# HGRN scores: the diagonal and the two smallest levels from one product over blocks of four tokens

## The chip, the cores and the metric

The kernel runs on one core of one Trainium2 chip. The time is device microseconds (us) of one launch; a kernel's time is the median of its runs. The engines are named PE (TensorE, matrix products), DVE (VectorE), ACT (ScalarE), POOL (GpSimd) and SP (SyncE, which issues the transfers).

## What is computed

One layer of a hybrid encoder over 16 learned tokens and 256 inputs (272 tokens, width 2048). After an RMSNorm, one projection `w_in` gives the inputs of two mixers: an HGRN2 gated linear recurrence (8 heads of 128) and a diagonal state-space model (S5, 64 groups). Both outputs are normed, joined and projected by `w_out`; a gated MLP with a short convolution and a last RMSNorm follow. The part that the change touches is the score matrix of the recurrence:

```python
f = lb + (1.0 - lb) * sigmoid(z); k = (1.0 - lb) * sigmoid(-z); q = silu(q)
b = cumsum(log(f))                                    # within a chunk
decay = exp(where(causal, b[t] - b[s], -inf))         # = product of f over s+1..t
scores[t, s] = sum_d q[t, d] * k[s, d] * decay[t, s, d]
o_intra = scores @ v
```

## The kernel before

All large products run on PE as three products of split operands (`mm3`, lines 184 to 186: high weights by high input, high by low, low by high). Weights come by DMA into `raw`, in units of 1 MB; `wsplit` makes of each unit two halves of 128x1024: `whi` on ACT (line 160) and `wlo` on DVE (the helper of line 82). Each half then feeds 24 products on PE, eight of them with `wlo`. There are three buffers each for `raw`, `whi` and `wlo`, so that PE can be at most about two halves behind the splits.

The columns of `w_in` are worked through in chunks in the order `u0 h0 u1 h1 u2 h2 u3 h3 g0 g1 g2 g3`. A `u` chunk feeds two S5 tiles (`s5_tile`, tiles `W`, `P`, `m`, `xo`, `bu`, `yps`). An `h` chunk gives two heads: `hg_f` makes the gates `f` (its tile is called `PP` in the profile) and `k`, `hg_q` makes `q`, `hg_i` makes `v`. `hg_group` then makes the 128x128 score blocks `S` (two heads by two blocks of 128 tokens, side by side in 512 columns), and `hg_cross` what crosses the blocks of 128.

`hg_group` never divides. It builds the scores in levels. The diagonal is taken from a product of `k` and `q` (PSUM tile `dps`), masked by the identity. Then, for h = 1, 2, 4, ... 64, blocks of 2h tokens are halved: queries of the right half, scaled by `f` (by then the running product of gates from the start of the half), meet keys of the left half, scaled by `SP` (the running product of gates up to the end of the half). `qh` and `kt` are the scaled operands, `lps` the PSUM tile of the product, and a predicated copy puts it into `S`. At the end of each level two DVE products double the reach of `SP` and of `f`. For h = 1 `SP` is still 1, so `k` itself is used and there is no `kt`.

The order of instructions on each engine is set when the kernel is built, by a scheduler that plays the program against a model of the engines' times, with priorities given in the code (`pri`): weight splits first, then the reading of accumulators, then the work of the heads. On the chip each engine takes its instructions in that fixed order and waits where an operand isn't there.

Of the kernel before, what the change touches and what calls it, by code (L numbers as in the profile page):

```python
# [9 lines left out]
F32 = mybir.dt.float32  # L10
F32R = mybir.dt.float32r
I32 = mybir.dt.int32
# [5 lines left out]
NM = 16  # L18
T = SEQ + NM
# [14 lines left out]
NQ = T - T0  # L34
# [5 lines left out]
NWARM2 = 10  # L40
LATE = 1.003
LEV = [1, 2, 4, 8, 16, 32, 64]

MAGIC = 12582912.0
LOG2E = 1.4426950408889634
# [7 lines left out]

def constants():
    ident = np.eye(128, dtype=np.float32)
    masks = np.zeros((128, len(LEV), 64), np.float32)
    s = np.arange(128)
    for l, h in enumerate(LEV):
        t = np.array([b * 2 * h + h + j for b in range(128 // (2 * h)) for j in range(h)])
        masks[:, l, :] = (s[:, None] // (2 * h) == t[None, :] // (2 * h)) & (s[:, None] % (2 * h) < h)  # L60
    misc = np.zeros((128, 26), np.float32)
    misc[:, 7] = 1.0
    misc[:, 15] = (s // S5H) % 2 == 0
    misc[:, 16] = (s // S5H) % 2 == 1
    misc[:, 17] = (s != NM - 1)
    misc[:, 18:26] = (s[:, None] % 32 == np.arange(NH)) & (s[:, None] < 64)
    return ident, masks.reshape(128, -1), misc
# [3 lines left out]
def hymba_kernel(ctx: ExitStack, tc: tile.TileContext, x, meta, lb_logits, norm_mix, w_in, hg_norm,  # L71
# [4 lines left out]
    act, dve, pool, pe, sp = nc.scalar, nc.vector, nc.gpsimd, nc.tensor, nc.sync  # L76
# [4 lines left out]
    def tt(dst, a, b, op, eng=dve):  # L81
        eng.tensor_tensor(out=dst, in0=a, in1=b, op=op)  # L82
# [21 lines left out]
    MUL, ADD, SUB, MAX, MIN = ALU.mult, ALU.add, ALU.subtract, ALU.max, ALU.min  # L104

    const = ctx.enter_context(tc.tile_pool(name="const", bufs=1))
# [3 lines left out]
    resp = ctx.enter_context(tc.tile_pool(name="res", bufs=1))  # L110

    ident = const.tile([128, 128], F32, name="ident")
    masks = const.tile([128, len(LEV), 64], F32, name="masks")
    misc = const.tile([128, 26], F32, name="misc")
    ones = const.tile([128, 128], F32, name="ones")
    onehot = misc[:, 0:15]
# [226 lines left out]
    def st(nm, p=prm, tag=None):  # L343
# [3 lines left out]
                    in_=lrow[64:96].unsqueeze(2).to_broadcast([32, 2, S5P]))  # L347
# [135 lines left out]
    for ri in range(2):  # L483
        for hb in range(2):
# [4 lines left out]
            for g in range(2):  # L489
                pr = slice(64 * g, 64 * g + 64)  # L490
                act.copy(out=cq[ri][pr, hb * 16:(hb + 1) * 16, :],
                         in_=tp[pr].rearrange("p b (j g h) -> p (b j) g h", g=2, h=S5H)[:, :, g])
# [20 lines left out]
    hgp = hgs.enter_context(tc.tile_pool(name="hg", bufs=1))  # L513
# [116 lines left out]
    oT = ogp.tile([128, NH, NQ], F32, tag="oT", name="oT")  # L630
    gs = ogp.tile([128, NH, NQ], F32, tag="gs", name="gs")
    kts = [hgp.tile([128, 4, 128], F32, name=f"kt{i}") for i in range(2)]
    for k in kts:
        pool.memset(k, 0.0)

    def hg_f(h0, accs):
# [39 lines left out]
            stt(gs[:, h0 + m], accs[m], vcol[:, V_HG + h0 + m:V_HG + h0 + m + 1], sg[:, m], MUL, MUL)  # L676

    def hg_group(h0, f, k, q, v, vm):
        S = hgp.tile([128, 4, 128], F32, tag="S", name="S")
        SP = hgp.tile([128, 2, T], F32, tag="SP", name="SP")  # L680
        pool.memset(SP, 1.0)
        ps = psc.tile([128, 4, 128], F32, tag="sc", name="dps")
        for m in range(2):
            for b in range(2):
                pe.matmul(ps[:, m * 2 + b], k[:, m, NM + 128 * b:NM + 128 * (b + 1)],
                          q[:, m, 2 + 128 * b:2 + 128 * (b + 1)], start=True, stop=True)
        tt(S, ps, ident.unsqueeze(1).to_broadcast([128, 4, 128]), MUL)
        q4 = q[:, :, 2:NQ]
        for l, h in enumerate(LEV):
            nb = 256 // (2 * h)  # L690
            qh = hgp.tile([128, 2, nb, h], F32, tag="qh", name="qh", bufs=3)
            tt(qh, q4.rearrange("p m (n s t) -> p m n s t", s=2, t=h)[:, :, :, 1],
               f[:, :, NM:T].rearrange("p m (n s t) -> p m n s t", s=2, t=h)[:, :, :, 1], MUL)
            if h == 1:
                lhs = [k[:, m, NM + 128 * b:NM + 128 * (b + 1)] for m in range(2) for b in range(2)]
            else:
                kt = kts[l % 2]
                tt(kt.rearrange("p (m b) t -> p m (b t)", b=2).rearrange("p m (n s t) -> p m n s t", s=2, t=h)[:, :, :, 0],
                   k[:, :, NM:T].rearrange("p m (n s t) -> p m n s t", s=2, t=h)[:, :, :, 0],
                   SP[:, :, NM:T].rearrange("p m (n s t) -> p m n s t", s=2, t=h)[:, :, :, 0], MUL)  # L700
                lhs = [kt[:, i] for i in range(4)]
            ps = psc.tile([128, 4, 64], F32, tag="sc", name="lps")
            qf = qh.rearrange("p m n t -> p (m n t)")
            if h >= 32:

                for b0 in range(0, 128, 2 * h):
                    for i in range(4):
                        pe.matmul(ps[b0:b0 + h, i, 0:h], lhs[i][:, b0:b0 + h],
                                  qf[:, 64 * i + b0 // 2:64 * i + b0 // 2 + h], start=True, stop=True)
                    act.copy(out=S[b0:b0 + h, :, b0 + h:b0 + 2 * h], in_=ps[b0:b0 + h, :, 0:h])  # L710
            else:
                for i in range(4):
                    pe.matmul(ps[:, i], lhs[i], qf[:, 64 * i:64 * (i + 1)], start=True, stop=True)  # L713
                nb1 = 128 // (2 * h)
                mk = masks[:, l].bitcast(I32).rearrange("p (n t) -> p n t", t=h)
                dve.copy_predicated(
                    out=S.rearrange("p b (n s t) -> p b n s t", s=2, t=h)[:, :, :, 1],
                    mask=mk.unsqueeze(1).to_broadcast([128, 4, nb1, h]),
                    data=ps.rearrange("p b (n t) -> p b n t", t=h))

            t0 = 0 if 2 * h <= NM else NM
            fv = f[:, :, t0:T].rearrange("p m (n s t) -> p m n s t", s=2, t=h)
            sv = SP[:, :, t0:T].rearrange("p m (n s t) -> p m n s t", s=2, t=h)
            n = (T - t0) // (2 * h)
            tt(sv[:, :, :, 0], sv[:, :, :, 0], fv[:, :, :, 1, h - 1:h].to_broadcast([128, 2, n, h]), MUL)
            tt(fv[:, :, :, 1], fv[:, :, :, 1], fv[:, :, :, 0, h - 1:h].to_broadcast([128, 2, n, h]), MUL)
        return S, SP

    def hg_cross(h0, f, f15, k, q, v, vm, S, SP):
        kx = hgp.tile([128, 2, 128], F32, tag="qh", name="kx", bufs=3)  # L730
        tt(kx, k[:, :, NM:NM + 128], SP[:, :, NM:NM + 128], MUL)
        km = hgp.tile([128, 2, NM], F32, tag="km", name="km")
        tt(km, k[:, :, 0:NM], SP[:, :, 0:NM], MUL)
        qm = hgp.tile([128, 2, NQ], F32, tag="qm", name="qm")
        qx = hgp.tile([128, 2, 128], F32, tag="qh", name="qx", bufs=3)
        tt(qm[:, :, 2:130], q[:, :, 2:130], f[:, :, NM:NM + 128], MUL)
        tt(qx, q[:, :, 130:NQ], f[:, :, NM + 128:T], MUL)
        tt(qm[:, :, 130:NQ], qx, f[:, :, NM + 127:NM + 128].to_broadcast([128, 2, 128]), MUL)
        tt(qm[:, :, 0:1], q[:, :, 0:1], f15, MUL)
        dve.tensor_copy(out=qm[:, :, 1:2], in_=q[:, :, 1:2])  # L740
        ps = psc.tile([128, 2, 128], F32, tag="sc", name="xps")
        for m in range(2):
            pe.matmul(ps[:, m], kx[:, m], qx[:, m], start=True, stop=True)
        sx = hgp.tile([128, 2, 128], F32, tag="sx", name="sx")
        act.copy(out=sx, in_=ps)
        sm = hgp.tile([NM, 2, NQ], F32, tag="iv", name="sm")
        for m in range(2):
            ps = psc.tile([128, NQ], F32, tag="sc", name="mps")
            pe.matmul(ps[0:NM], km[:, m], qm[:, m], start=True, stop=True)
            act.copy(out=sm[:, m, 1:NQ], in_=ps[0:NM, 1:NQ])  # L750
            ts(sm[:, m, 0:1], ps[0:NM, 0:1], misc[0:NM, 17:18], MUL)
        for m in range(2):
            ps = psc.tile([128, NQ], F32, tag="sc", name="ops")
            pe.matmul(ps, vm[:, m], sm[:, m], start=True, stop=False)
            pe.matmul(ps[:, 2:130], v[:, 2 * m], S[:, 2 * m], start=False, stop=False)
            pe.matmul(ps[:, 130:NQ], v[:, 2 * m], sx[:, m], start=False, stop=False)
            pe.matmul(ps[:, 130:NQ], v[:, 2 * m + 1], S[:, 2 * m + 1], start=False, stop=True)
            act.copy(out=oT[:, h0 + m], in_=ps)
# [57 lines left out]
    for c in range(4):  # L816
# [3 lines left out]
        with pri(-3):  # L820
            for m in range(2):
                j = 2 * c + m
                sg = tlp.tile([128, NQ], F32, tag="sq", name="sgl", bufs=3)
# [67 lines left out]
    for c in range(8):  # L891
# [3 lines left out]
        for m in range(2):  # L895
            kt = 2 * c + m
# [21 lines left out]
    for c in range(FF // 256):  # L918
        accs = [pf.tile([128, NQ], F32, tag="f", name="ga") for _ in range(2)]
        mm3(accs, [(wunit(colunit(w_gate, k, c)), k * 8) for k in range(2)], ffr, 0, NQ)  # L920
        for m in range(2):
            j = 2 * c + m
            a = fw.tile([128, NQ], F32, tag="a", name="a", bufs=2)
            b = fw.tile([128, SEQ], F32, tag="b", name="b", bufs=2)
# [23 lines left out]
    for t in range(2):  # L948
        for n in range(4):
            for k in range(4):  # L950
                kt = n * 4 + k
                pe.matmul(dps[t][n][:, k * 128:(k + 1) * 128], hT[:, kt, 2 + t * 128:2 + (t + 1) * 128], ident,
                          start=(k == 0), stop=False, is_transpose=True, skip_group_check=True)
# [18 lines left out]
    for j in range(KF - NT):  # L972
        a = act_split(j)
# [73 lines left out]
```

## Time and profile before

| | |
|---|---|
| runs | 1252.16, 1253.86, 1254.13 us; median 1253.86 us |
| the profiled execution's own time | 1252.36 us |
| its span, first to last instruction | 1250.6 us |
| busy share of the span | PE 98%, DVE 70%, ACT 48%, POOL 9% |
| mean granted TensorE clock | 0.994 |

In the profile's rows a line number is followed by the engine, the operation, the tiles (written tile, arrow, read tiles) and the shape. Many DVE operations come from helpers: line 82 is any product or difference of two tensors, so the tiles tell which it is. A product of two float32 operands on PE stands as two records. Two DVE records that follow each other overlap by some tens of nanoseconds, so what an instruction costs the queue is the distance from its start to the next start. The four heads' groups run between about 65 and 360 us of the span; the MLP fills the span from about 520 us on.

### The profile page before, as it was taken

Reading aid. Unit: us, or ns where it says so; the run is one execution under the profiler, and the core shown is the slowest. Engines: PE = TensorE matmul, PEld = TensorE weight load, DVE = VectorE, ACT = ScalarE, POOL = GpSimd, SP = SyncE. Lnnn points to the kernel's source line nnn. Section 1 sums busy time; section 2 is a strip of 40 time slices with the busy share of each in tenths; the row PEclk is TensorE's granted clock in tenths of the full one; section 3 lists DMA queues with packets and bytes.
Section 4 is the critical chain, followed back from the end, with each engine's and each line's share of the span. In section 5 each row is a group of like instructions: output and inputs, shape, how many; then the busy total and the mean of one; then the engine's idle time right before and its main releaser. Section 6 shows DMA issues by size and latency. Waiting matters only on the chain.

```text
span 1250.6 us, 22795 instructions
## 1 busy us (share of the span) xinstructions
PE 1226.9 (98%) x9299; PEld 1151.9 (92%) x9299; DVE 873.7 (70%) x1516; ACT 601.2 (48%) x1042; POOL 117.0 (9%) x165
## 2 busy tenths in 40 slices
PE   7989999999999999999999999999999999999997
PEld 6979898989989999999999999999999988888886
DVE  8989999999748867765665656656656645554554
ACT  5646767574545446343433433433434434444454
POOL 5483132221000000000000000000000000000000
PEclk9989999999999999999999999999999999999999
DMA  8533344243444565565556555555555545555552
GB/s 256 147 122 113 105 144 136 86 134 127 144 135 136 169 201 172 167 203 179 192 172 199 171 196 173 193 178 187 184 181 191 210 166 198 202 188 187 197 205 98
DMA packets 176298, 210.82 MB, mean 169 GB/s; under 512 B 14773, under 2 KB 168880, under 8 KB 170416
## 3 DMA queue, kind: packets, MB, share of 16 engines
q1 hardware_dynamic: 175871, 209.26, 51.1%
q8 instruction: 73, 1.20, 0.4%
q14 instruction: 34, 0.27, 0.1%
q0 software_dynamic: 320, 0.09, 0.0%
HBM read 206.12 MB, written 2.10 MB: 166 GB/s over the span
## 4 chain that ended last, share of the span: by engine, by line
PE 92%; DVE 3%; POOL 2%; issue 1%; DMA 1%; ACT 0%; SPq 0%; DVEq 0%; ACTq 0%; POOLq 0%
PE acc L186 9%; PE acc L184 8%; PE acc L185 8%; PE ua L185 7%; PE ua L184 7%; PE ga L184 7%; PE ua L186 7%; PE ga L186 7%; PE ga L185 7%; PE d L970 6%; PE d L969 6%; PE d L968 6%; PE lps L713 1%; PE bu L600 1%; DVE xn L91 1%
## 5 line engine op out<-in xcount | busy, mean ns | idle before, releaser
L82 DVE TENSOR_TENSOR wlo<-raw,whi 128x1024 fp32r<-128x1024 f32 (+1 forms) x376 | 461.4, 1227 | 320.8 <-ACT whi L160 271.2
L160 ACT CAST whi<-raw 128x1024 fp32r<-128x1024 f32 (+1 forms) x382 | 397.8, 1042 | 519.9 <-PE ga L185 158.3
L184 PE MATMUL ga<-fh,whi 128*128 128x258 f32 x704 | 199.0, 283 | 0.5 <-DVE a L82 0.5
L186 PE MATMUL ga<-fh,wlo 128*128 128x258 f32 x704 | 198.5, 282 | 0.0
L185 PE MATMUL ua<-fl,whi 128*128 128x256 f32 x704 | 198.4, 282 | 0.0
L185 PE MATMUL ga<-fl,whi 128*128 128x258 f32 x704 | 198.1, 281 | 0.0
L186 PE MATMUL ua<-fh,wlo 128*128 128x256 f32 x704 | 197.9, 281 | 0.0
L184 PE MATMUL ua<-fh,whi 128*128 128x256 f32 x704 | 197.9, 281 | 0.0
L186 PE MATMUL acc<-xh,wlo 128*128 128x272 f32 (+1 forms) x640 | 186.7, 294 | 5.0 <-DVE wlo L82 5.0
L185 PE MATMUL acc<-xl,whi 128*128 128x272 f32 (+1 forms) x640 | 186.1, 292 | 3.9 <-DVE xl L82 3.9
L184 PE MATMUL acc<-xh,whi 128*128 128x272 f32 (+1 forms) x640 | 186.4, 294 | 0.4 <-ACT PP L79 0.4
L184 PEld LDWEIGHTS ga<-fh,whi 128*128 128x128 f32 x704 | 133.0, 189 | 0.7 <-DVE a L82 0.7
L185 PEld LDWEIGHTS ga<-fl,whi 128*128 128x128 f32 x704 | 133.5, 190 | 0.0
L184 PEld LDWEIGHTS ua<-fh,whi 128*128 128x128 f32 x704 | 133.1, 189 | 0.0
L186 PEld LDWEIGHTS ua<-fh,wlo 128*128 128x128 f32 x704 | 132.9, 189 | 0.0
L185 PEld LDWEIGHTS ua<-fl,whi 128*128 128x128 f32 x704 | 132.8, 189 | 0.0
L186 PEld LDWEIGHTS ga<-fh,wlo 128*128 128x128 f32 x704 | 132.6, 189 | 0.0
L186 PEld LDWEIGHTS acc<-xh,wlo 128*128 128x128 f32 x640 | 121.4, 190 | 9.4 <-DVE wlo L82 5.6
L185 PEld LDWEIGHTS acc<-xl,whi 128*128 128x128 f32 x640 | 121.6, 190 | 7.5 <-DVE xl L82 4.8
L968 PE MATMUL d<-whi,ah 128*128 128x512 f32 x328 | 127.7, 389 | 0.0
L969 PE MATMUL d<-whi,al 128*128 128x512 f32 x328 | 127.6, 389 | 0.0
L184 PEld LDWEIGHTS acc<-xh,whi 128*128 128x128 f32 x640 | 121.1, 190 | 4.1 <-issue 2.0
(381 smaller groups left out, 1868.1 us busy)
## 6 DMA issues: line engine op xcount, KB each, us to landing
raw<-in_w_ffn_gate SPq DMA_DIRECT2D x44, 1024.0 KB, 5.1
raw<-in_w_ffn_up SPq DMA_DIRECT2D x44, 1024.0 KB, 5.1
raw<-in_w_ffn_down SPq DMA_DIRECT2D x44, 1024.0 KB, 4.8
raw<-in_w_in SPq DMA_DIRECT2D x39, 1024.0 KB, 5.2
raw<-in_w_out SPq DMA_DIRECT2D x16, 1024.0 KB, 5.8
raw<-in_w_glu SPq DMA_DIRECT2D x4, 1024.0 KB, 5.2
x<-in_x SPq DMA_DIRECT2D x4, 512.0 KB, 5.7
out<-ob SPq DMA_DIRECT2D x8, 256.0 KB, 2.7
```

Of the source, the lines that this page charges most:

```text
L82: eng.tensor_tensor(out=dst, in0=a, in1=b, op=op)
L91: dve.scalar_tensor_tensor(out=dst, in0=a, scalar=s, in1=b, op0=op0, op1=op1, **kw)
L160: act.copy(out=hi[:, c], in_=raw[:, hf, c])
L184: pe.matmul(accs[m], lh, xh[:, n0:n1], start=first, stop=False)
L185: pe.matmul(accs[m], lh, xl[:, n0:n1], start=False, stop=False)
L186: pe.matmul(accs[m], ll, xh[:, n0:n1], start=False, stop=end)
L600: return pe.matmul(bus[i][:, ri], bt[h, 2 * ri + q0 // 2], R[h, q0 // 2], start=True, stop=True)
L713: pe.matmul(ps[:, i], lhs[i], qf[:, 64 * i:64 * (i + 1)], start=True, stop=True)
L968: pe.matmul(dps[t][n], ah[:, tk], hi, start=False, stop=False, skip_group_check=True)
L969: pe.matmul(dps[t][n], al[:, tk], hi, start=False, stop=False, skip_group_check=True)
L970: pe.matmul(dps[t][n], ah[:, tk], lo, start=False, stop=end, skip_group_check=True)
```

## The change

Diagonal, h = 1 and h = 2 become one product. `f` and `SP` are first widened twice (`widen(1)`, `widen(2)`), so that they hold running products within blocks of four tokens. All keys are scaled by `SP` into `kt` (512 columns), all queries by `rv`, the reciprocal of `SP`, into `qt`; inside a block of four, the ratio of two suffix products is the product of the gates between the two tokens. One product of `kt` and `qt` fills `dps`, and one predicated copy with a causal mask of four-token blocks puts it into `S`. The levels h = 4 to 64 stay. The first `SP` is copied from `f` on ACT in place of a DVE product with ones; `S` is one tile that POOL clears once; the mask constant has five in place of seven blocks of 64 columns. `rv` and `qt` lie in the buffers of `qm` and `sg`.

```diff
-    masks = np.zeros((128, len(LEV), 64), np.float32)
+    masks = np.zeros((128, 5, 64), np.float32)
+    masks[:, 0:2] = ((s[:, None] // MBLK == s[None, :] // MBLK) & (s[:, None] <= s[None, :])).reshape(128, 2, 64)
...
-    for k in kts:
+    S = hgp.tile([128, 4, 128], F32, name="S")
+    for k in kts + [S]:
         pool.memset(k, 0.0)
...
+        def widen(h):
+            t0 = 0 if 2 * h <= NM else NM
+            fv, sv = halves(f, h, t0), halves(SP, h, t0)
+            n = (T - t0) // (2 * h)
+            if h == 1:
+                act.copy(out=sv[:, :, :, 0], in_=fv[:, :, :, 1])
+            else:
+                tt(sv[:, :, :, 0], sv[:, :, :, 0], fv[:, :, :, 1, h - 1:h].to_broadcast([128, 2, n, h]), MUL)
+            tt(fv[:, :, :, 1], fv[:, :, :, 1], fv[:, :, :, 0, h - 1:h].to_broadcast([128, 2, n, h]), MUL)
+        widen(1)
+        widen(2)
+        kt = kts[0]
+        qt, rv = (hgp.tile([128, 2, 256], F32, tag=t_, name=n_) for t_, n_ in (("sg", "qt"), ("qm", "rv")))
+        dve.reciprocal(out=rv, in_=SP[:, :, NM:T])
+        tt(kt.rearrange("p (m b) t -> p m (b t)", b=2), k[:, :, NM:T], SP[:, :, NM:T], MUL)
+        tt(qt, q[:, :, 2:NQ], rv, MUL)
         ps = psc.tile([128, 4, 128], F32, tag="sc", name="dps")
         for m in range(2):
             for b in range(2):
-                pe.matmul(ps[:, m * 2 + b], k[:, m, NM + 128 * b:NM + 128 * (b + 1)],
-                          q[:, m, 2 + 128 * b:2 + 128 * (b + 1)], start=True, stop=True)
-        tt(S, ps, ident.unsqueeze(1).to_broadcast([128, 4, 128]), MUL)
-        for l, h in enumerate(LEV):
+                pe.matmul(ps[:, m * 2 + b], kt[:, m * 2 + b], qt[:, m, 128 * b:128 * (b + 1)], start=True, stop=True)
+        dve.copy_predicated(out=S, mask=masks[:, 0:2].bitcast(I32).rearrange("p a t -> p (a t)").unsqueeze(1)
+                            .to_broadcast([128, 4, 128]), data=ps)
+        for l, h in enumerate((4, 8, 16, 32, 64)):
...
-            if h == 1:
-                lhs = [k[:, m, NM + 128 * b:NM + 128 * (b + 1)] for m in range(2) for b in range(2)]
...
+            widen(h)
```

The scheduler gives every engine a new order. Three places matter below.

DVE in the first group (h0), before: from the second `q` to the next weight split. `sca`, `cpc` and `ew` are set-up of the S5 part.

```order
L91 SCALAR_TENSOR_TENSOR q<-acc,lbc,sg 128x258
L82 TENSOR_TENSOR cpc<-sca 128x32x16
L82 TENSOR_TENSOR qh<-q,PP 128x256
L82 TENSOR_TENSOR qm<-q,f_1196 128x2
L740 COPY qm<-q 128x2
L82 TENSOR_TENSOR sca<-scb,zai 128x512
L82 TENSOR_TENSOR sca<-scb,zar 128x512
L82 TENSOR_TENSOR PP<-PP 128x272
L472 COPY ew<-pw 128x32 x3
L82 TENSOR_TENSOR wlo<-raw,whi 128x1024
```

The same place after the change:

```order
L94 SCALAR_TENSOR_TENSOR q<-acc,lbc,sg 128x258
L85 TENSOR_TENSOR cpc<-sca 128x32x16
L85 TENSOR_TENSOR PP<-PP 128x136x2
L705 RECIPROCAL rv<-SP 128x512
L85 TENSOR_TENSOR kt_610<-k,SP 128x512
L85 TENSOR_TENSOR kt_611<-k,SP 128x64x4
L85 TENSOR_TENSOR sca<-scb,zai 128x512
L85 TENSOR_TENSOR sca<-scb,zar 128x512
L85 TENSOR_TENSOR qh<-q,PP 128x256
L475 COPY ew<-pw 128x32 x2
L85 TENSOR_TENSOR wlo<-raw,whi 128x1024
```

The reciprocal and two `kt` products now stand ahead of that split; two small operations on `qm` are gone from there, and `qh` is now that of h = 4.

DVE in the second group (h1), after the change, between two weight splits:

```order
L85 TENSOR_TENSOR wlo<-raw,whi 128x1024
L85 TENSOR_TENSOR PP<-PP 128x136x2
L705 RECIPROCAL rv<-SP 128x512
L85 TENSOR_TENSOR kt_610<-k,SP 128x512
L85 TENSOR_TENSOR kt_611<-k,SP 128x64x4
L85 TENSOR_TENSOR P<-W,m 128x544
L85 TENSOR_TENSOR ysb<-ysb,gq 128x2x129
L94 SCALAR_TENSOR_TENSOR W<-W,pw,tmp 128x2x34
L85 TENSOR_TENSOR P<-W,bu 128x544
L85 TENSOR_TENSOR wlo<-raw,whi 128x1024
```

Eight instructions stand between the two splits, the reciprocal among them.

PE in the first group, before, around the first piece of `dps`:

```order
L185 MATMUL acc<-xl,whi 128x272
L186 MATMUL acc<-xh,wlo 128x272
L685 MATMUL dps<-q,k 128x128 x2
L184 MATMUL acc<-xh,whi 128x272
L185 MATMUL acc<-xl,whi 128x272
```

And after the change, where `dps` now stands: behind the first products with the `wlo` that the DVE rows above end with (the row ahead of `dps` belongs to the unit after it).

```order
L188 MATMUL acc<-xl,whi 128x272
L711 MATMUL dps<-qt,kt_610 128x128 x4
L189 MATMUL acc<-xh,wlo 128x272
L187 MATMUL acc<-xh,whi 128x272
L188 MATMUL acc<-xl,whi 128x272
```

Its two pieces, which stood ahead of that `wlo` among products of earlier halves, are now one piece behind it.

More of the change, by code (lines that the diff above doesn't have):

```diff
@@ L42 @@
 LEV = [1, 2, 4, 8, 16, 32, 64]
+MBLK = 4
 MAGIC = 12582912.0
@@ L55, in constants @@
     ident = np.eye(128, dtype=np.float32)
-    masks = np.zeros((128, len(LEV), 64), np.float32)
+    masks = np.zeros((128, 5, 64), np.float32)
     s = np.arange(128)
-    for l, h in enumerate(LEV):
+    masks[:, 0:2] = ((s[:, None] // MBLK == s[None, :] // MBLK) & (s[:, None] <= s[None, :])).reshape(128, 2, 64)
+    for l, h in enumerate((4, 8, 16)):
         t = np.array([b * 2 * h + h + j for b in range(128 // (2 * h)) for j in range(h)])
-        masks[:, l, :] = (s[:, None] // (2 * h) == t[None, :] // (2 * h)) & (s[:, None] % (2 * h) < h)
+        masks[:, 2 + l, :] = (s[:, None] // (2 * h) == t[None, :] // (2 * h)) & (s[:, None] % (2 * h) < h)
     misc = np.zeros((128, 26), np.float32)
@@ L112, in hymba_kernel @@
     ident = const.tile([128, 128], F32, name="ident")
-    masks = const.tile([128, len(LEV), 64], F32, name="masks")
+    masks = const.tile([128, 5, 64], F32, name="masks")
     misc = const.tile([128, 26], F32, name="misc")
@@ L678, in hg_group, with halves @@
     def hg_group(h0, f, k, q, v, vm):
-        S = hgp.tile([128, 4, 128], F32, tag="S", name="S")
         SP = hgp.tile([128, 2, T], F32, tag="SP", name="SP")
         pool.memset(SP, 1.0)
+        def halves(a, h, t0=NM):
+            return a[:, :, t0 - (T - a.shape[2]):].rearrange("p m (n s t) -> p m n s t", s=2, t=h)
+        def widen(h):
[14 more added lines that the diff above has]
+        tt(qt, q[:, :, 2:NQ], rv, MUL)
         ps = psc.tile([128, 4, 128], F32, tag="sc", name="dps")
@@ L684, in hg_group @@
             for b in range(2):
-                pe.matmul(ps[:, m * 2 + b], k[:, m, NM + 128 * b:NM + 128 * (b + 1)],
-                          q[:, m, 2 + 128 * b:2 + 128 * (b + 1)], start=True, stop=True)
-        tt(S, ps, ident.unsqueeze(1).to_broadcast([128, 4, 128]), MUL)
-        q4 = q[:, :, 2:NQ]
-        for l, h in enumerate(LEV):
+                pe.matmul(ps[:, m * 2 + b], kt[:, m * 2 + b], qt[:, m, 128 * b:128 * (b + 1)], start=True, stop=True)
+        dve.copy_predicated(out=S, mask=masks[:, 0:2].bitcast(I32).rearrange("p a t -> p (a t)").unsqueeze(1)
+                            .to_broadcast([128, 4, 128]), data=ps)
+        for l, h in enumerate((4, 8, 16, 32, 64)):
             nb = 256 // (2 * h)
             qh = hgp.tile([128, 2, nb, h], F32, tag="qh", name="qh", bufs=3)
-            tt(qh, q4.rearrange("p m (n s t) -> p m n s t", s=2, t=h)[:, :, :, 1],
-               f[:, :, NM:T].rearrange("p m (n s t) -> p m n s t", s=2, t=h)[:, :, :, 1], MUL)
-            if h == 1:
-                lhs = [k[:, m, NM + 128 * b:NM + 128 * (b + 1)] for m in range(2) for b in range(2)]
[L696 to L701, printed above, removed]
+            tt(qh, halves(q, h)[:, :, :, 1], halves(f, h)[:, :, :, 1], MUL)
+            kt = kts[(l + 1) % 2]
+            tt(halves(kt.rearrange("p (m b) t -> p m (b t)", b=2), h)[:, :, :, 0],
+               halves(k, h)[:, :, :, 0], halves(SP, h)[:, :, :, 0], MUL)
             ps = psc.tile([128, 4, 64], F32, tag="sc", name="lps")
@@ L707, in hg_group @@
                     for i in range(4):
-                        pe.matmul(ps[b0:b0 + h, i, 0:h], lhs[i][:, b0:b0 + h],
+                        pe.matmul(ps[b0:b0 + h, i, 0:h], kt[:, i, b0:b0 + h],
                                   qf[:, 64 * i + b0 // 2:64 * i + b0 // 2 + h], start=True, stop=True)
@@ L712, in hg_group @@
                 for i in range(4):
-                    pe.matmul(ps[:, i], lhs[i], qf[:, 64 * i:64 * (i + 1)], start=True, stop=True)
+                    pe.matmul(ps[:, i], kt[:, i], qf[:, 64 * i:64 * (i + 1)], start=True, stop=True)
                 nb1 = 128 // (2 * h)
-                mk = masks[:, l].bitcast(I32).rearrange("p (n t) -> p n t", t=h)
+                mk = masks[:, 2 + l].bitcast(I32).rearrange("p (n t) -> p n t", t=h)
                 dve.copy_predicated(
@@ L719, in hg_group @@
                     data=ps.rearrange("p b (n t) -> p b n t", t=h))
[L721 to L726, printed above, removed]
+            widen(h)
         return S, SP
```

## The prediction

> **What bounds the kernel now.** I read the page first, then busy time by stretch, then what PE waited for.
>
> ```profile
> PE 1226.9 (98%) x9299; PEld 1151.9 (92%) x9299; DVE 873.7 (70%) x1516; ACT 601.2 (48%) x1042; POOL 117.0 (9%) x165
> ```
>
> ```profile
> 100.00:300.00 200.00, 200.00 (x1787) 181.30 (x1787) 193.53 (x421) 132.12 (x376) 54.81 (x63) 1.00 0.39 119
> 300.00:400.00 100.00, 100.00 (x810) 92.00 (x808) 72.09 (x134) 49.23 (x87) 1.14 (x2) 1.00 0.46 148
> 81.00:89.50 8.50, 8.50 (x48) 8.00 (x49) 7.82 (x16) 6.48 (x19) 5.72 (x11) 0.50 0.58 179
> ```
>
> The columns of the second fence are the stretch, its length, then busy time of PE, PE's weight loads, DVE, ACT and POOL, and the granted clock. In the stretch where the heads are worked, 100 to 300 us, PE is never idle, but DVE has only 200 - 193.5 = 6.5 us free. In the next 100 us it has 27.9. So two engines are nearly full at once, and the question is which of them sets the pace. The view of PE's waits from 28 to 420 us answers it:
>
> ```profile
> PE acc L186 <- DVE wlo L82: 5.2, 4, 3.6
> PE dps L685 <- DVE q L91: 0.6, 1, 0.6
> ```
>
> Between 90 and 404 us the same view names no wait of PE at all. PE sets the pace, and DVE keeps just ahead of it. The one large wait lies in the first group:
>
> ```profile
> 77.08 0.29 PE L185 MATMUL acc<-xl,whi 128*128 128x272 f32 x1
> 80.97 0.60 PE L186 MATMUL acc<-xh,wlo 128*128 128x272 f32 x1 [3.61 <-DVE wlo L82]
> ```
>
> After it PE runs at half clock until about 89.5 us (the 0.50 above). Anything that makes PE's list shorter behind 81 us is gained in full; anything that keeps DVE from that split at 80 us is lost in full.
>
> **What PE saves.** Each group loses two levels of four products (h = 1, h = 2), eight records each. One level in the second group:
>
> ```profile
> 155.92 0.29 PE L184 MATMUL acc<-xh,whi 128*128 128x272 f32 x1
> 156.05 1.00 PE L713 MATMUL lps<-qh,k 128*128 128x64 f32 x8
> 156.86 0.38 PE L185 MATMUL acc<-xl,whi 128*128 128x272 f32 x1
> 157.07 0.29 PE L186 MATMUL acc<-xh,wlo 128*128 128x272 f32 x1
> ```
>
> 156.05 to 156.86 is 0.81 us, and the product behind it takes 0.21 us to its successor, where the one ahead takes 0.13: 0.89 us a level. Eight levels: 7.1 us. `dps` stays as four products of the same shape. In the first group, however, its two pieces stood ahead of the long wait, where PE's time was free:
>
> ```profile
> 68.67 0.60 PE L685 MATMUL dps<-q,k 128*128 128x128 f32 x4
> 69.03 0.37 PE L184 MATMUL acc<-xh,whi 128*128 128x272 f32 x1
> ```
>
> 0.36 us and the same 0.08 for the product behind, twice. Now they stand behind the wait: +0.9 us.
>
> **What DVE pays.** Of the reciprocal there are only small ones; of the rest there are rows of the same kind.
>
> ```profile
> L780 DVE RECIPROCAL f<-PP 128x2 f32<-128x2 f32 x4 | 0.6, 150 | 0.0
> L439 DVE RECIPROCAL lq<-lq 128x8 f32<-128x8 f32 x1 | 0.2, 191 | 0.0
> L414 DVE RECIPROCAL den<-den 128x32 f32<-128x32 f32 x1 | 0.3, 347 | 0.0
> ```
>
> ```profile
> 153.38 0.68 DVE L82 TENSOR_TENSOR S<-dps,ident 128x512 f32<-128x512 f32 x1
> 153.98 0.24 DVE L91 SCALAR_TENSOR_TENSOR W<-W,pw,tmp 128x34 f32<-128x34 f32 x1
> ...
> 154.48 0.41 DVE L82 TENSOR_TENSOR qh<-q,PP 128x256 f32<-128x256 f32 x1
> 154.81 0.43 DVE L82 TENSOR_TENSOR SP<-SP,PP 128x272 f32<-128x272 f32 x1
> 155.16 0.43 DVE L586 TENSOR_TENSOR_SCAN m<-r,m 128x136 f32<-128x136 f32 x1
> ...
> 157.85 0.41 DVE L82 TENSOR_TENSOR kt<-k,SP 128x256 f32<-128x256 f32 x1
> 158.19 0.71 DVE L82 TENSOR_TENSOR P<-W,m 128x544 f32<-128x544 f32 x1
> ...
> 160.59 0.73 DVE L716 COPY_PREDICATED S<-masks,lps 128x256 f32<-128x256 int32 x1
> 161.12 0.47 DVE L82 TENSOR_TENSOR qh<-q,PP 128x256 f32<-128x256 f32 x1
> ```
>
> From start to start a group loses: `S` from `dps` 0.60, two predicated copies 1.06, two `qh` 0.66, one `kt` 0.34, the first `SP` 0.35; together 3.0 us. It gains `kt` and `qt` of 512 columns (0.60 each, as the `S` product), a predicated copy of 512 columns (between 0.60, the `S` product, which also reads 512 columns of PSUM, and 1.06, twice the row; I take 0.60) and the reciprocal. The three reciprocals lie on one line: (347 - 191) / 24 = 6.5 ns and (191 - 150) / 6 = 6.8 ns for each further column. So 512 columns take 347 + 480 x 6.5 = 3.47 us. The lower bound is the 0.60 of a product, if a long one ran at that pace; the upper is the whole 347 ns scaled by 16, 5.55 us. I take 3.4 in the queue, because the slope holds twice. DVE's account is then +5.2 - 3.0 = +2.2 us a group, 8.8 us in four. It is covered by the 6.5 us free until 300 us and the 27.9 us behind; without that cover all 8.8 would be PE's wait.
>
> [...]
>
> **Where that lands in the first group.** The rows of DVE ahead of the late split:
>
> ```profile
> 70.66 1.76 DVE L82 TENSOR_TENSOR wlo<-raw,whi 128x1024 fp32r<-128x1024 f32 x1
> ...
> 72.74 0.68 DVE L82 TENSOR_TENSOR cpc<-sca 128x512 f32<-128x512 f32 x1
> 73.34 0.42 DVE L82 TENSOR_TENSOR qh<-q,PP 128x256 f32<-128x256 f32 x1
> ...
> 73.93 1.58 DVE L82 TENSOR_TENSOR sca<-scb,zai 128x512 f32<-128x512 f32 x1
> 75.44 1.58 DVE L82 TENSOR_TENSOR sca<-scb,zar 128x512 f32<-128x512 f32 x1
> 76.95 0.56 DVE L82 TENSOR_TENSOR PP<-PP 128x272 f32<-128x272 f32 x1
> 78.94 0.86 DVE L472 COPY ew<-pw 128x32 f32<-128x32 f32 x3 [1.43 <-POOL pw L82]
> 79.70 1.21 DVE L82 TENSOR_TENSOR wlo<-raw,whi 128x1024 fp32r<-128x1024 f32 x1
> ```
>
> and POOL and ACT rows that the walk and the next part use:
>
> ```profile
> 51.59 0.30 POOL L82 TENSOR_TENSOR pt<-pw 128x64 f32<-128x64 f32 x1 [11.06 <-DVE pw L82]
> ...
> 73.89 2.58 POOL L82 TENSOR_TENSOR scb<-ew,pw 128x512 f32<-128x512 f32 x2
> ...
> 85.15 0.36 ACT L658 COPY iv<-acc 128x272 f32<-128x272 f32 x1
> ```
>
> By the new order: up to 73.34 as now (one `kt` is gone ahead of it, two half-size products come); `PP` 0.36, reciprocal 3.4, `kt` 0.60 and 0.34 end at 78.0; then two `sca`. These took 1.51 us each beside POOL's row of 73.89; undisturbed they are 0.60 like `S`. Then `qh` 0.33, two `ew` about 0.5, the split 1.14. It ends at 81.2 with quick `sca` and 83.0 with slow ones, against 80.84. DVE's 1.43 us of waiting for POOL and POOL's drag on `sca` are what covers most of the reciprocal. I take the middle, 82.1: PE resumes 1.3 us later. Bounds: with a reciprocal of 0.60 the split waits for POOL as it does now, 0; with 5.55 it is 3.4.
>
> **Edits that cost nothing.** POOL's clearing of `S` comes once, ahead of the 11.06 us in which POOL waits for DVE; without that wait it would hold POOL for some tenths of a us. The copy of the first `SP` moves to ACT, 132 of 200 us busy, four times about the 0.36 us of the row above; the next `PP` product waits for it, and behind that the reciprocal, so an ACT queue that is late by 1 us would cost 1 us in the first group alone. The mask transfer shrinks. `qt` in the buffer of `sg` and `rv` in that of `qm` add waits on readers that are done microseconds earlier.
>
> **Later groups.** In h1 the row of instructions shown in the order is 0.35 + 3.4 + 0.60 + 0.34 + 0.63 + 0.34 + 0.2 + 0.63 + 1.13 = 7.6 us from split to split, where PE uses up a half in 24 x 0.13 = 3.1 us. The lead there is, from the end of a split to its first product (eight such products a half, counted in order):
>
> ```profile
> 137.72 1.22 DVE L82 TENSOR_TENSOR wlo<-raw,whi 128x1024 fp32r<-128x1024 f32 x1
> ...
> 145.22 0.29 PE L186 MATMUL acc<-xh,wlo 128*128 128x272 f32 x1
> ```
>
> That is 145.22 - 138.94 = 6.3 us. 6.3 + 3.1 - 7.6 leaves 1.8, so PE doesn't wait; the scheduler has moved S5 work behind. Cost: 0, with 1.8 us to spare.
>
> **Sum.** -7.1 + 0.9 + 1.3 = -4.9 us: 1247.5 us for the profiled execution, whose own 1252.36 lies 1.5 below the median of the runs shown. Against the median of 1253.86: 1249.0 us.
>
> **Rivals.**
> A. *DVE's lead isn't there* (the other side). Were the lead in h1 to h3 only what it is in the first group, where the split of 70.66 ends at 72.42 and is first used at 73.67 (row below), then 7.6 - 3.1 - 1.25 = 3.25 us of waiting in each of three groups, 9.75 us: -4.9 + 9.75 = +4.85, 1258.7 us. The change is slower if the lead falls below 4.5 - 4.9 / 3 = 2.9 us. For it: DVE has 6.5 free of 200 us. Against: the 6.3 measured at this place.
>
> ```profile
> 73.67 0.29 PE L186 MATMUL acc<-xh,wlo 128*128 128x272 f32 x1
> ```
>
> B. *The half clock lasts longer.* In the trace it ends 8.5 us after PE resumes. If the later resumption cost another such stretch at half speed, 4.25 us: -0.65, 1253.2 us. For it: PE stands still longer, since `dps` no longer breaks the wait. Against: the stretch may simply move with the resumption. [...]
> C. *The reciprocal is quick* (0.60 us): no later split, -7.1 + 0.9 = -6.2, 1247.7 us. Against: the slope.
> D. *The splits set the pace* and PE's shorter list only becomes waiting: the first split's +1.3 remains (1255.2 us), and DVE's 8.8 come on top as far as the free 6.5 us don't take them, 2.3: 1257.5 us. For it: DVE is busy 97% of 100 to 300 us. Against: no wait of PE between 90 and 404 us.
>
> **How the numbers follow.** About 0.2% (2.5 us) is what a measurement of this kernel can tell from no change. Forecast 0.58; A 0.11, B 0.13, C 0.10, D 0.08. Faster: nearly all of the forecast (0.56), C, and a small part of B (0.03): 0.69. Slower: A and most of D (0.07): 0.18. Same: the rest, 0.13, most of it B. The range: at the low end C's 1247.7 less 1.7, the distance of the fastest of the three runs from their median: 1246.0. At the high end it takes in B, and the forecast with the reciprocal's upper bound and a wait of one group: 1249.0 + 2.1 + 3.25 = 1254.4. A and D (0.19) lie outside.
>
> **What would show it.** Right: the two levels gone from PE's records, PE without waits from about 92 to 404 us, one reciprocal of about 3.5 us a group, PE's long wait ending at 81 to 83 us, DVE busier by some 9 us before 360. Wrong: waits of PE for `wlo` in h1 to h3 (A, D), half clock past 90 us (B), reciprocals below 1 us (C).

## The result, and the profile after

The changed kernel took 1246.05 us in the median (1245.26 to 1247.16, four runs) against 1253.04 us before (1252.16 to 1254.13, four runs): a ratio of 0.9944, 95% interval 0.9927 to 0.9962. It is 7.0 us faster; 4.9 had been forecast. The profiled execution took 1245.69 us, 6.67 less than that of before. Of the experiments below, one run of `pin_copy` (1595.42 us) and one of `pin_warm` (2387.4 us) were slow; without them their medians are 1245.10 and 1245.19 us, and the ratios leave them out.

The page's first part, busy time with its share and the number of instructions:

```profile
PE 1219.3 (98%) x9235; PEld 1144.6 (92%) x9235; DVE 881.3 (71%) x1504; ACT 601.2 (48%) x1046; POOL 116.9 (9%) x166
```

PE has 64 records and 7.6 us less, DVE 7.6 us more. Busy time by stretch, for the same three stretches as before (stretch, length, PE, weight loads, DVE, ACT, POOL, granted clock):

```profile
81.00:89.50 8.50, 7.04 (x40) 7.04 (x41) 7.76 (x16) 3.90 (x13) 6.92 (x11) 0.63 0.62 205
100.00:300.00 200.00, 200.00 (x1767) 182.70 (x1766) 194.16 (x391) 130.39 (x357) 48.93 (x59) 1.00 0.40 125
300.00:400.00 100.00, 99.81 (x809) 89.33 (x807) 81.77 (x162) 53.78 (x116) 6.45 (x6) 1.00 0.42 133
```

PE is still never idle from 100 to 300 us. DVE's added work shows from 300 to 400: 81.8 us instead of 72.1; from 100 to 300 it is 0.6 us more. In the first stretch the clock is 0.63 instead of 0.50. What PE waited for, from 28 to 420 us:

```profile
PE acc L189 <- DVE wlo L85: 7.3, 4, 6.4
PE acc L188 <- DVE xl L85: 2.2, 2, 1.7
PE acc L187 <- ACT PP L82: 0.4, 1, 0.4
```

The one long wait is still that of the first group, 6.4 us instead of 3.6. Between 90 and 404 us the view names only one wait, of 0.2 us, at 398, in another stage. The rows of DVE and PE around the long wait:

```profile
73.79 3.34 DVE L705 RECIPROCAL rv<-SP 128x512 f32<-128x512 f32 x1
77.06 2.04 DVE L85 TENSOR_TENSOR kt<-k,SP 128x512 f32<-128x512 f32 x2
79.02 0.88 DVE L85 TENSOR_TENSOR sca<-scb,zai 128x512 f32<-128x512 f32 x1
79.82 0.69 DVE L85 TENSOR_TENSOR sca<-scb,zar 128x512 f32<-128x512 f32 x1
...
81.19 1.21 DVE L85 TENSOR_TENSOR wlo<-raw,whi 128x1024 fp32r<-128x1024 f32 x1
```

```profile
75.80 0.29 PE L188 MATMUL acc<-xl,whi 128*128 128x272 f32 x1
82.46 0.59 PE L189 MATMUL acc<-xh,wlo 128*128 128x272 f32 x1 [6.37 <-DVE wlo L85]
...
87.96 1.06 PE L711 MATMUL dps<-qt,kt 128*128 128x128 f32 x8
```

The reciprocal takes 3.34 us, the `sca` products behind it run at 0.7 to 0.9 us (POOL's `scb` row is over by 76.6 us), and PE resumes at 82.46 us. `dps` follows behind the wait.

**Where the time went.** Two tables are worked out from the rows of PE. The first gives the time from each product's start to the next one's, added up by the tile written (a wait counts to the product ahead of it), from the 145th to the 2065th weight product (about 44 to 390 us); the second how much later than in the kernel before the n-th weight product (counted from 0) starts:

```
us by tile written     before   after  pe_only  pin_copy  pin_warm
weight products (acc)  261.29  261.75   261.19    261.01    254.34
lps                     23.16   15.59    15.46     15.59     15.60
dps                      3.01    3.52     3.18      3.52      3.52
all else                59.00   58.55    58.84     58.55     65.27
sum                    346.46  339.41   338.67    338.67    338.73
```

```
n (time in before)      after  pe_only  early_b  early_r34
 144  (43.7 us)         +0.35    +1.17    +0.69     +1.26
 288  (64.4 us)         +0.21    +1.17    +0.53     +1.51
 432  (98.5 us)         -1.71    -2.86   -11.90    -10.59
1968 (378.1 us)         -6.70    -6.62    -5.96    -11.53
2352 (430.1 us)         -6.70    -6.63    -7.45    -11.76
last (1225.9 us)        -6.71    -6.66    -7.36    -11.81
```

(In `pin_warm`, experiment 4, all else holds the products added there. Between the rows shown the second table can mislead, since the heads' products stand in other places among the weight products.) The whole gain is there by 378 us and nothing changes behind it. It is `lps`, 7.6 us. Of these, 1.1 us belong to the half clock: in the kernel before, the h = 1 level of the first group ran in it and took 1.90 us from start to start, where the level in the forecast's rows took 0.81:

```profile
84.57 1.97 PE L713 MATMUL lps<-qh,k 128*128 128x64 f32 x8
86.47 0.45 PE L550 MATMUL ktp<-cp,eb 128*32 128x32 f32 x12
```

The weight products cost about the same in sum, because the longer wait (+2.8 us) is balanced by shorter ones ahead of it (-0.8), by less half clock behind it (-0.7) and by 0.8 less further on, where fewer of them stand behind a level. The clock record of the traces has the half clock in steps of 3.41 us (three before, two after), which the expectations call windows:

```
half clock from 76 to 92 us    from    to     length  PE's wait ahead of it
before                         79.48   89.72   10.24   3.6
after                          80.42   87.25    6.83   6.4
pe_only                        81.36   88.19    6.83   3.6
no_recip                       84.79   88.20    3.41   1.7 and 2.8
bwarm                          81.47   91.71   10.24   2.8
pin_copy                       79.52   86.35    6.83   5.8
warm, pin_warm                 none             0      1.2, 1.3
```

### The profile page after: what moved, and what is told of

Same layout as the page of the kernel before. It is cut to its first block, busy times and chain, and to the rows that moved or that the text cites. A ratio compares the mean times of both kernels' runs of the same rounds, so it can differ in the third digit from the quotient of the medians.

```text
span 1243.9 us, 22660 instructions
## 1 busy us (share of the span) xinstructions
PE 1219.3 (98%) x9235; PEld 1144.6 (92%) x9235; DVE 881.3 (71%) x1504; ACT 601.2 (48%) x1046; POOL 116.9 (9%) x166
## 4 chain that ended last, share of the span: by engine, by line
PE 94%; DVE 4%; DMA 0%; issue 0%; ACT 0%; SPq 0%; DVEq 0%; ACTq 0%
PE acc L189 9%; PE acc L187 9%; PE acc L188 9%; PE ua L188 7%; PE ua L187 7%; PE ga L187 7%; PE ua L189 7%; PE ga L189 7%; PE ga L188 7%; PE d L983 6%; PE d L981 6%; PE d L982 6%; PE bu L603 1%; PE lps L732 1%; DVE wlo L85 1%; DVE xn L94 1%
```

## The experiments

Theory P is the forecast's: PE's list sets the time, and only the first group's late split holds it up. The rivals are D (DVE's splits set the pace), O (the gain is a matter of the new order) and H, on the clock: the half clock explains what the sum lacked.

**1. Only PE's products taken out of the kernel before** (`pe_only`).

```diff
-            ps = psc.tile([128, 4, 64], F32, tag="sc", name="lps")
+            if h > 2:
+                ps = psc.tile([128, 4, 64], F32, tag="sc", name="lps")
...
-                for i in range(4):
+                for i in range(4 if h > 2 else 0):
                     pe.matmul(ps[:, i], lhs[i], qf[:, 64 * i:64 * (i + 1)], start=True, stop=True)
```

The predicated copies of h = 1 and 2 stay and read the product of the diagonal, so the scores of these levels are left out.

> The kernel before without the products of the two smallest levels: VectorE does all it did before (the queries, keys and both predicated copies, which now read the diagonal's products, so the scores of h = 1 and h = 2 are left out). Theory P: 1253.04 - 7.1 = 1245.9 us, all of the change's gain without its VectorE work; the long wait of the first group ends at about 81.0 us as before. Rival O or D (the order, or the splits on VectorE, set the pace): about 1253 us, since VectorE's work is the same. If the forecast's split of the sum is right (-7.1 for PE, +0.9 and +1.3 paid back in the first group), this kernel is about 2.2 us faster than the changed one would be at the same half clock, 1243.8 to 1245.9 us.

1245.42 us, ratio 0.9944 (0.9931 to 0.9958): all of the gain, with the DVE work of before.

```profile
PE 1220.9 (98%) x9235; PEld 1145.4 (92%) x9235; DVE 871.5 (70%) x1516; ACT 601.9 (48%) x1042; POOL 116.9 (9%) x165
```

So the gain is PE's list, not DVE's work. O isn't excluded by this run alone, since the planner gave it an order of its own. Its half clock was one step shorter than before although its wait is the same 3.6 us, only 1.2 us later. It was expected to be 2.2 us faster than the changed kernel and was 0.6 faster; in its profile it had lost 0.8 us more than the changed kernel ahead of the first row of the second table.

**2. The products put back into the changed kernel**, as two sets that nothing reads: once in the planner's order (`pe_back`), once with every instruction of the changed kernel held in its place (`pin_back`). The lines that hold the order are left out here and below.

```diff
+        for _ in range(2):
+            ps = psc.tile([128, 4, 64], F32, tag="sc", name="lps")
+            for i in range(4):
+                pe.matmul(ps[:, i], kt[:, i], qt[:, i // 2, 128 * (i % 2):128 * (i % 2) + 64], start=True, stop=True)
         for l, h in enumerate((4, 8, 16, 32, 64)):
```

> The changed kernel with two sets of four products a group added again, of the shape of the two levels taken out (128 x 64), whose results nothing reads. VectorE's work is as in the changed kernel. Theory P (PE's list sets the time): the changed kernel's 1246.05 us plus eight levels of 0.89 us = +7.1, so 1253.2 us, level with the kernel before; PE records back from 9235 to about 9299. Rival O (the gain came from the other order the planner made, or from work VectorE lost): 1246 us, the added products lie in gaps. The stretch at half clock behind the first long wait may move either by one window of 3.4 us, which is worth 1.7 us.

> The changed kernel with its issue order fixed on every engine, instruction by instruction, and the two unread sets of four products put in ahead of each group's first lps product; nothing else differs. Theory P: 1246.05 + 8 x 0.89 = 1253.2 us (with the 0.95 us a level that the records show, 1253.6). Then the 4 us that the same products cost beyond this in the planner's own order came from that order. Rival: such products cost more than their records, 1257.5 us as there.

1257.51 us (ratio 1.0043, 1.003 to 1.0055) and 1258.94 us (1.0053, 1.004 to 1.0065): 11.5 and 12.9 above the changed kernel, more than any theory had. `pin_back` shows a fault of the experiment. The unread products read `kt`, which DVE overwrites two levels on, so DVE waited for them; what DVE waited for from 84 to 400 us, and the first case:

```profile
DVE kt L124 <- PE lps L756: 18.2, 4, 5.4
```

```profile
93.44 0.43 DVE L124 TENSOR_TENSOR kt<-k,SP 128x256 f32<-128x256 f32 x1 [3.74 <-PE lps L756]
```

They also share the single PSUM buffer of `lps`, and its hand-over from one set to the next adds to them (PE waited 0.8 us in two places for DVE's copy out of it): `lps` costs 9.5 us more by the first table's reckoning, not 7.1. The rest, some 4 us, are waits of PE and the products' neighbours. In `pe_back`, where DVE waits only 0.3 us for them, `lps` costs 7.3 us more, as P has it, and the other 3 us came with its order and stay unexplained. So an order of the planner's may be worth some 3 us here; no run shows that apart. One thing `pin_back` shows unasked: 18.2 us of standing on DVE cost PE no more than 4 us.

**3. Is DVE felt?** The reciprocal left out in the planner's order (`no_recip`), replaced by a copy in the fixed order (`pin_copy`), and doubled in h1 to h3 (`recip2`).

```diff
-        dve.reciprocal(out=rv, in_=SP[:, :, NM:T])
         tt(kt.rearrange("p (m b) t -> p m (b t)", b=2), k[:, :, NM:T], SP[:, :, NM:T], MUL)
-        tt(qt, q[:, :, 2:NQ], rv, MUL)
+        tt(qt, q[:, :, 2:NQ], SP[:, :, NM:T], MUL)
```

> The changed kernel without its reciprocals: the queries are multiplied by the suffix products themselves, so the inverse is left out (3.34 us of VectorE less in each of four groups). Theory P: in h1 to h3 nothing is won, since PE doesn't wait there; in the first group the split comes when POOL lets it, as in the kernel before, so PE resumes at about 81.0 instead of 82.46 us: -1.5 us, 1244.6 us. Rival D (VectorE sets the pace): 3.34 us in each group, -13 us, 1233 us. Rival O: the order changes again, with no sign foreseen.

```diff
-        dve.reciprocal(out=rv, in_=SP[:, :, NM:T])
+        dve.tensor_copy(out=rv, in_=SP[:, :, NM:T])
```

> The changed kernel, issue order fixed, with a plain copy of 512 columns in place of each reciprocal: the inverse is left out, VectorE has some 2.7 us less in each group. Theory P: in h1 to h3 nothing is won. In the first group the split can come when the copies that wait for POOL let it, at about 80.3 instead of 81.2 us, so PE resumes 0.9 to 1.5 us earlier: 1244.5 to 1245.2 us. The half clock behind it may be one window of 3.4 us longer or shorter, 1.5 us either way. Rival D: 2.7 us in each of four groups, 1235 us.

```diff
-        dve.reciprocal(out=rv, in_=SP[:, :, NM:T])
+        for _ in range(1 if h0 == 0 else 2):
+            dve.reciprocal(out=rv, in_=SP[:, :, NM:T])
```

> The changed kernel with the reciprocal done twice in h1, h2 and h3 (3.34 us of VectorE more in each, the first group unchanged). In the changed kernel the shortest distances from the end of a split to its first product are 2.33 us in h1 and 2.48 us in h2. Theory P with these leads: the splits come up to 3.34 us later, so PE waits about 1.0 us in each of the three groups, +3 us at most, 1246 to 1249 us; waits of PE for wlo appear between 130 and 290 us. Rival D (VectorE sets the pace already): +10 us, 1256 us. Third possibility, the planner moves the added time where nothing waits: 1246.0 us and no new wait.

`no_recip` took 1246.29 us (0.9948, 0.9936 to 0.9961), no gain over the changed kernel (in its profile 2.4 us more were lost ahead of the 145th weight product, so it says little of DVE), `pin_copy` 1245.17 us (0.9943, 0.9929 to 0.9957), `recip2` 1247.11 us (0.9961, 0.9948 to 0.9973). D had 1233 to 1235 and 1256. In `pin_copy` the n-th weight product comes 0.60 us earlier than in the changed kernel at n = 432 and 0.61 earlier at n = 2352: 2.9 us less of DVE's work in each of h1, h2 and h3 (a copy of 0.42 in place of 3.34 us) are worth nothing. The 0.6 us are the first group's, less than the 0.9 expected. Its DVE rows:

```profile
73.97 0.53 DVE L748 COPY rv<-SP 128x512 f32<-128x512 f32 x1
...
75.48 1.57 DVE L128 TENSOR_TENSOR sca<-scb,zai 128x512 f32<-128x512 f32 x1
76.98 1.57 DVE L128 TENSOR_TENSOR sca<-scb,zar 128x512 f32<-128x512 f32 x1
...
80.44 0.47 DVE L518 COPY ew<-pw 128x32 f32<-128x32 f32 x2 [1.43 <-POOL pw L128]
80.81 1.23 DVE L128 TENSOR_TENSOR wlo<-raw,whi 128x1024 fp32r<-128x1024 f32 x1
```

What the copy saves goes into slower `sca` products (1.57 instead of 0.69 to 0.88 us; the kernel before had 1.58 beside POOL's `scb`) and into the old wait for POOL, 1.43 us. `recip2` has 3.34 us more in three groups and costs about 1 us in the median; its only wait of PE for a weight split between 90 and 404 us is this:

```profile
PE acc L189 <- DVE wlo L85: 0.3, 1, 0.3
```

The leads of 2.3 us alone would have made waits of 1 us each; in the planner's new order they didn't come.

**4. The half clock.** Products that nothing reads keep PE busy in the long wait: in the planner's order (`bwarm` in the kernel before, `warm` in the changed one) and in the fixed order of the changed kernel (`pin_warm`). The lines that hold them in their place are left out here; they use the PSUM buffer of `dps`.

```diff
+            wk = psc.tile([128, 128], F32, tag="sc", name="wk")
+            for _ in range(23):                            # 12 in bwarm, 20 in warm
+                pe.matmul(wk, ident, ident, start=True, stop=True)
```

> The kernel before with twelve products of 128 x 128 that nothing reads, queued on PE right ahead of the product that waits for the late split of the first group (some 3.2 of the 3.6 us of that wait). They hold the buffer of dps, so its first use moves behind the wait (+0.9 us). Theory H (the half clock behind the wait is paid because PE stands still): the clock stays at 1.00 from 76 to 92 us and the 4.5 us above the usual pace that the trace of before shows from 80 to 90 us go: 1252.4 - 4.5 + 0.9 = 1248.8 us. Rival: the half clock comes anyway, 1253.3 us.

> The changed kernel with twenty such products in the same place (5.3 of the 6.4 us of its wait). Theory H: the 2.2 to 2.3 us above the usual pace that its trace shows from 82 to 87 us go: 1246.05 - 2.2 = 1243.8 us. The difference to the kernel before with its twelve is then the forecast's sum without any half clock, -7.1 + 1.5 = -5.6 us (both have dps behind the wait): that the change measured -7.0 and not -4.9 us lies in the half clock. Rival: the difference stays -7 us, and the missing 2.1 us are elsewhere.

> The changed kernel, issue order fixed, with 23 products of 128 x 128 that nothing reads directly ahead of the product that waits in the first group (about 6.1 of its 6.4 us). Theory H: PE resumes at 82.5 us as before, but at full clock: the 2.3 us of half clock go, 1243.8 us, and the profile shows no window of half clock between 76 and 92 us. Then the forecast without the half clock is tested: -7.1 + 0.9 + 1.5 = -4.7 us against a kernel before whose own three windows are taken off (1252.36 - 4.5). Rival: half clock comes anyway, 1246.0 us.

`bwarm` took 1253.34 us (1.0007, 0.9998 to 1.0016), `warm` 1245.22 (0.9937, 0.9925 to 0.995), `pin_warm` 1245.52 (0.9942, 0.9928 to 0.9955). Busy time from 76 to 92 us, of `bwarm` and then of `pin_warm`:

```profile
76.00:92.00 16.00, 12.34 (x81) 11.48 (x80) 11.97 (x24) 8.03 (x28) 12.29 (x19) 0.68 0.40 131
```

```profile
76.00:92.00 16.00, 14.74 (x135) 14.14 (x133) 15.41 (x26) 6.62 (x22) 12.54 (x19) 1.00 0.40 132
```

`bwarm` failed as an experiment: its split came later and 2.8 us of wait were left, and the clock was halved for 10.24 us as in the kernel before. Its difference to `warm` tells nothing of the sum. `pin_warm` did what it should: no half clock (1.00 in the mean from 76 to 92 us, where the changed kernel has 0.79), and at n = 384 its weight products, counted from their own start at n = 288, are 1.8 us ahead of the changed kernel's (2.3 expected). But 1.0 us of that is gone again by n = 816, half of it where in h1 PE now comes early to a DVE result,

```profile
PE acc L231 <- DVE q L137: 0.5, 1, 0.5
```

and 0.7 us is left at the end. H is confirmed for the place and the rough size; a gain there isn't kept whole, and `warm` and `pin_warm` stay about 1.5 us above the 1243.8 us expected.

**5. The late split queued early**, in the kernel before (`bearly`) and in the changed one (`early_b`; with the reciprocal over three of four columns, `early_r34`). `hold` adds an edge that orders the issue alone. The lines that collect `cts`, `splits`, `ews` and `rvs` are left out here; in `early_r34` `rv` has a buffer of its own, which POOL sets to 1 once.

```diff
+                for p in cts[2:]:                          # the two last sca products
+                    hold(p, splits[d0])                    # behind the late split
+                with tc.issue_after(splits[d0].ins):
                     S, SP = hg_group(2 * g, f, k, q, v, vm)
...
+            for p in ews:                                  # the copies that wait for POOL
+                hold(p, splits[d0 + 2])
+            if rvs:
+                hold(rvs[0], splits[d0 + 1])               # the first reciprocal
```

```diff
-        dve.reciprocal(out=rv, in_=SP[:, :, NM:T])
+        dve.reciprocal(out=rv.rearrange("p m (b t) -> p m b t", t=MBLK)[:, :, :, 0:MBLK - 1],
+                       in_=halves(SP, 2).rearrange("p m n s t -> p m n (s t)")[:, :, :, 0:MBLK - 1])   # early_r34
```

> The kernel before with the late split of the first group queued on VectorE ahead of the two coefficient products, the copies that wait for POOL and the rest of the first group's work (issue order alone; the same instructions). Theory P: PE's wait of 3.8 us and the 4.5 us of half clock behind it both go, 1252.4 - 8.3 = 1244.1 us. Against it: the work that is put off comes back as waits later, in the worst case all of it, 1252.4 us.

> The changed kernel with the same order of the split, and its first reciprocal behind the split after that. Theory P: the wait of 6.5 us and the 2.2 us of half clock go: 1246.05 - 8.7 = 1237.3 us. Its difference to the kernel before with the same order is then PE's list alone: eight levels taken out, the dps products the same, -7.1 to -7.6 us. Rival D (VectorE sets the pace once the wait is gone): the 8.8 us more of VectorE's work come back as waits in h0 to h3, 1241 to 1246 us.

> The changed kernel with the first group's late split queued early, as in the run that had this alone (1245.04 us, where 4.0 us came back as PE's wait for gh at 360 us), and with the reciprocal over three of every four columns: the suffix product of a block's last token is 1 and its inverse is set once. VectorE saves 128 of 512 columns, 0.84 us a group at 6.5 ns each, 3.3 us in all, and the planner puts the last yps further ahead of gh. Theory: the wait for gh falls below 1 us, 1240 to 1241.5 us. Rival (VectorE's total work sets the end of this stretch): 3.3 us of the 4.0 at most, 1241.7 us; or the wait only moves, 1245 us.

`bearly` took 1249.7 us (0.9976, 0.9967 to 0.9986), `early_b` 1245.04 (0.9935, 0.9923 to 0.9948), `early_r34` 1240.64 (0.9904, 0.9889 to 0.9919). In all three the long wait and its half clock are gone (the longest wait of PE between 75 and 90 us is 0.9, 2.0 and 0.9 us); at n = 432 `early_b` is 11.9 us ahead of the kernel before. In `early_b` most of what is lost of this comes back at one place, PE's wait from 90 to 390 us for the end of the S5 part, with one step of half clock behind it (364.94 to 368.35 us):

```profile
PE acc L195 <- ACT gh L847: 3.8, 1, 3.8
```

Here DVE does set an end: with PE 10 us earlier, the S5 chain that runs through DVE is last, and its last `yps` stood only 27 weight products ahead of `gh`. `early_r34` makes the reciprocal shorter

```profile
L715 DVE RECIPROCAL rv<-SP 128x384 f32<-128x384 f32 x4 | 10.2, 2539 | 0.0
```

and the planner put the last `yps` 77 products ahead; from 90 to 390 us no wait of PE is left, and it is the fastest version, 11.8 us under the kernel before. Which of the two, the 3.2 us of DVE or the place of `yps`, brought it wasn't taken apart. `bearly` is 6.5 us ahead of the kernel before at n = 432 and 2.6 at n = 2352, so more than half was lost again, in pieces that the view of waits doesn't name; that stays open.

## Why the prediction was right, and where its size was off

The mechanism was right, and the time lies 3 us under the forecast, only 0.05 us inside the low end of the range, which is luck. Of the 3 us, 0.8 are the kernel before, whose median came out at 1253.04 us where the forecast had 1253.86. Term by term, from the profiled executions:

| term | forecast | measured |
|---|---|---|
| eight levels on PE | -7.1 | -7.1 (`lps` 23.16 to 15.59, without the 1.1 of the level in the half clock; 0.08 for the product behind each, as the forecast has it) |
| `dps` behind the wait | +0.9 | +0.9 (87.96 to 88.77 us, and 0.08 behind) |
| PE resumes later | +1.3 | +1.5 (80.97 to 82.46), 0.35 of it from the start |
| half clock behind the wait | 0 | -2.2 (4.5 to 2.3) |
| all else | 0 | +0.2 |
| sum | -4.9 | -6.7 |

- **The step that failed** is the half clock. The sum left it as it was, and rival B, the only place where it was spoken of, gave it a plus sign. PE's products ran 4.5 us over their usual pace between the wait and 90 us before (weight products 3.0, start to start less 0.126 us each; the `lps` level 1.1; `ktp` 0.4) and 2.3 after, though PE stood still longer. The table of half clocks shows why the wait alone gave no sign: 10.24 us behind waits of 3.6 and 2.8 us, 6.83 behind 3.6, 5.8 and 6.4. It comes in steps of 3.41 us that don't start with the wait: the wait before began at 77.36 us and the half clock at 79.48, after at 76.09 and 80.42. A step costs, as an estimate, 3.41 x (1 - 0.126 / 0.226) = 1.5 us, at 0.226 us a weight product in the half clock of both traces against 0.126 outside it. Across runs, of 37 runs of the kernel before taken with the experiments, the 11 with a mean clock of 0.991 or less have a median of 1253.64 us, the 21 with 0.994 or more 1251.41; the mean doesn't say where in the span the half clock lay. So a part of the measured 7.0 may be chance, and the forecast should have held a bound of one step on both sides.
- **A rival to chance that no run tests.** In each of the ten traces with half clock between 75 and 400 us, it ends with a step in which PE didn't stand still and spent 2.9 to 3.4 of the 3.41 us on weight products. The earlier steps of half clock hold at least 0.5 us of standing still, but for one: the kernel before's step from 82.89 to 86.31, in which PE had work throughout, 1.7 us of it the `lps` level of h = 1 and 0.35 `ktp`. The change takes that level out, and `pe_only`, which lacks it too, has one step less. So the third step may be owed to the level and not to chance; then up to 1.5 us more of the gain is the change's own. That is argued from rows, not shown.
- A step of half clock in which PE had work throughout was followed by the full clock in the changed kernel (busy from 83.84, full clock at 87.25) and not in the one before, where PE was busy from 82.89 to 86.31 and the clock stayed halved until 89.72.
- **The reciprocal** was sized right by the slope of the small rows (3.4 taken, 3.34 measured), and with it the later split; rival C falls. By 512 and 384 columns it is (3342 - 2539) / 128 = 6.3 ns a column, where the small rows had 6.5 and 6.8.
- **Rival A and rival D** fall: no wait in h1 to h3, and 2.9 us a group taken from DVE there moved nothing (`pin_copy`). What DVE had more, 7.6 us by the busy times where 8.8 had been forecast, was hidden, as forecast, by time that lay free mostly behind 300 us. D returns only once the long wait is gone (`early_b`).
- The other seven levels that were taken out took 0.75 to 1.03 us of their own, 0.86 in the mean, where the row of the forecast had 0.81; the levels that stay took 0.35 us more in sum than before. The two about cancel, so the sum of this term fits better than its parts.

## What to carry to other kernels

When one engine has no wait for hundreds of microseconds, price a change by what leaves that engine's list, and ask of the other engines only how far ahead they are; a stall ahead of it can cost more than itself, since here half clock came with it (in the kernel before, a wait of 3.6 us and 4.5 us over the usual pace behind it), in steps of 3.41 us whose number the length of the stall didn't tell, so give such a term a range of one step each way. If the long wait can be taken away, do that first, and then look again for what is late next: here it was the other full engine, at a place 280 us further on. A probe that adds instructions must not read a buffer that the program reuses, or it measures its own wait; holding every other instruction in its place makes such a fault visible.

## What the runs showed of the hardware

Behind 75 us, waits of PE of 1.2, 1.3 and 2.0 us left the clock at 1.00 (`warm`, `pin_warm`, and `early_b` at 89 us); waits of 2.8 to 6.4 us had 3.41 to 10.24 us of half clock in them or behind them, and the longest stretch of it, 10.24 us, came with waits of 2.8 and 3.6 us, not with the longest. Near 28 us, a wait of 1.85 us left it at 1.00 in the kernel before, and one of 1.75 us in the changed kernel had a step of half clock behind it (29.22 to 32.63). A DVE product of 512 columns (`sca`) took 0.88 and 0.69 us in the changed kernel, beside POOL rows of at most 256 columns (78.78 to 81.15 us), and 1.58 for each of the two that the kernel before ran from 73.9 to 77.0 us, mostly beside POOL's `scb` rows of 512 columns (73.89 to 76.47 us; two others there, at 68.9 and 69.9 us beside rows of 64 to 256 columns, took 1.15 and 0.80); in `pin_copy` it took 1.57 twice, so work that was saved on DVE came back as slower work.
